# A Strassen-Winograd encoder layer on one core: the plain chunks become pairs, and the gathering bank begins with a copy

## The chip, the core and the metric

The kernel runs on one core of a Trainium2 chip. Its time is the device time of one execution in microseconds (us). TensorE (PE) does the matrix products, into eight PSUM banks of 128 x 512 float32. VectorE (DVE) and ScalarE (ACT) move and combine results, SyncE (SP) and GpSimd (POOL) issue DMAs.

## The reference

One post-norm encoder layer on x of 1024 x 1024, float32:

```
h = LN1(alpha*x + 0.5*SwiGLU_a(x))          # SwiGLU(x) = (silu(x Wg) * (x Wu)) Wd, width 2752
h = LN2(alpha*h + Mixer(h))
h = LN3(alpha*h + 0.5*SwiGLU_b(h))
# Mixer: one projection -> q, k, v (12 heads of 128), Fourier channels, gates;
#   dilated window attention in 3 head groups + FFT over positions and channels,
#   each projected, gated, summed, one output projection
```

## The kernel before

Every large float32 product is made from parts: `split` rounds an operand on ACT ("hi"), DVE subtracts to get the rest ("lo"), and three matmuls (hi hi, hi lo, lo hi) give one. A **product** is 12 matmuls of 128 x 128 by 128 x 512: four slices of a 512-long inner dimension, three matmuls each.

A **pair** is two chunks of 128 weight columns (gate and up, or q and k) against all rows. It is a 2 x 2 block product, made the Strassen-Winograd way with 7 products for 8 (`PROD`): a11 b11, a12 b21, s4 b22, a22 t4, s1 t1, s2 t2, s3 t3. The s are sums of x's blocks, made once per part by `Operand.derive`; the t are sums of the pair's weight blocks, made on DVE by `pair_weights` (t12 and t34). `ORDER` is the order on TensorE: 1, 6, 2, 7, 5, 4, 3. Bank A takes 1 and 2, bank B takes 6, 7 and 4, bank D takes 5 and 3. `pair_sums` copies product 1 to SBUF on ACT (r1, L501) after product 1, and DVE adds it to bank B after product 6 (r2, L505) and after product 7 (r3, L509). `after` finishes a feed-forward pair: silu of bank A (L587), sum of bank B and r1 on DVE (L593), its silu, two subtractions and two multiplications. `pair_out` does the same for the mixer's pairs, where attention runs beside them.

The first two chunks of each feed-forward part are **plain**: 8 products each (`plain`), first four per chunk on the upper half of the rows (a11, a12), then four on the lower half, so that the sums of x are needed only after 18 products. Products 1 and 2 of the first pair stand between the halves. Then come 19 pairs, a 64-column tail, and the down projection (L741, L763), also Strassen-Winograd.

After the first part and after the output projection come layer norms by row tile (`norm_nodes`): deviation and root on ACT (L896, L898), then two DVE passes, (y + mean) * gain (L903) and * 1/std + offset (L907). The row is stored for later and transposed on TensorE; ACT copies the transpose out of PSUM (L382), with 256 columns per instruction, into the blocks of the next operand. The last norm stores to the output, its last row tile in two halves.

A planner (`Flow`) sets the order on each engine while the program is written: TensorE's jobs stand in the order written by hand, and DVE's, ACT's and the queues' instructions are placed by costs, due times (`need`, `lead`) and free buffers: 46 pages of 128 x 1024, 11 halves, 8 banks. `Q` is a load, `S` an ACT and `V` a DVE task, `F` a TensorE step that goes between jobs when ready. Every engine then runs its list in order.

## Time and profile before

| | us |
|---|---|
| median of 3 runs | 2091.3 (2090.82 to 2091.37) |
| profiled execution | 2091.71 |
| its span | 2089.9 |
| TensorE busy | 2071.5 |
| DVE, ACT, POOL busy | 1371.5, 773.3, 237.3 |
| DMA moved | 378.20 MB, mean 181 GB/s |

Busy time of TensorE is that of matmuls as the profile models them. The waits view lists, for an engine, who was waited for: us in total, times, longest. The chain view follows the work that ended last. In the windows view each engine's busy time stands with its count of instructions, then the granted clock as a share, the DMA share and GB/s. A timeline row is start, duration, engine, line, operation, out<-in, and in brackets the idle time before it and what ended it.

### The profile page before, as it was taken

The numbers are of one execution on the slowest core, as the hardware profiler recorded it, in microseconds if no ns is written. First come the engines' busy times: TensorE is split into PE (matmuls) and PEld (weight loads), VectorE is DVE, ScalarE is ACT, GpSimd is POOL, SyncE is SP. The second block draws the span as 40 slices with busy tenths as digits, with TensorE's granted clock in tenths as the row PEclk, the third lists the DMA queues.
The fourth block names the chain that finished last, engine by engine and source line by source line (L and its number), as shares of the span: only waits on it lengthen the run. The fifth ranks groups of instructions, "written<-read, shape, count | busy, mean of one in ns | idle before, by whom it ended". The sixth has DMA issues, their size and how long they took to land.

```text
span 2089.9 us, 25459 instructions
## 1 busy us (share of the span) xinstructions
PE 2071.5 (99%) x9571; PEld 1724.3 (83%) x9571; DVE 1371.5 (66%) x1879; ACT 773.3 (37%) x1181; POOL 237.3 (11%) x415
## 2 busy tenths in 40 slices
PE   9999999999999999999999999999999999999998
PEld 7888888888888888888888888888788888888886
DVE  6766766676675668556666664857766666675566
ACT  4322222355453212444445433225332222245332
POOL 0222111111000010022132101000001001010000
PEclk9999999999999999999999999999999999999999
DMA  4679766499843336567875439432223223267653
GB/s 171 198 215 304 225 179 187 154 335 405 290 165 121 111 111 177 184 152 204 235 177 163 173 131 348 171 122 111 76 91 130 82 91 136 89 233 271 235 179 106
DMA packets 143740, 378.20 MB, mean 181 GB/s; under 512 B 18291, under 2 KB 40563, under 8 KB 143169
## 3 DMA queue, kind: packets, MB, share of 16 engines
q1 hardware_dynamic: 105600, 251.70, 34.3%
q0 software_dynamic: 38016, 124.88, 20.6%
q8 instruction: 75, 1.23, 0.2%
q14 instruction: 49, 0.39, 0.1%
HBM read 288.72 MB, written 145.45 MB: 208 GB/s over the span
## 4 chain that ended last, share of the span: by engine, by line
PE 97%; issue 1%; DVE 1%; ACT 0%; DMA 0%; SPq 0%; DVEq 0%
PE Bb L422 7%; PE Ba L422 7%; PE Aa L422 5%; PE Ab L422 5%; PE Db L422 5%; PE Da L422 5%; PE Bq L422 5%; PE Dq L422 3%; PE Aq L422 3%; PE Bs L422 3%; PE Zb L741 3%; PE Xb L741 3%; PE Za L741 3%; PE Xa L741 3%; PE wo L1910 3%; PE pj L1823 2%
## 5 line engine op out<-in xcount | busy, mean ns | idle before, releaser
L1405 ACT ACTIVATE p<-p,stat 128x192 f32<-128x192 f32 (+2 forms) x96 | 42.3, 442 | 24.7 <-DVE stat L1400 24.0
L533 POOL DMA_DIRECT2D hsba<-r2b x19 | 10.3, 541 | 330.3 <-DVE r2b L603 312.0
L1392 DVE SCALAR_TENSOR_TENSOR p<-sc,bias 128x512 f32<-128x512 f32 (+1 forms) x40 | 24.8, 620 | 27.9 <-PE sc L1378 21.6
L1437 PEld LDWEIGHTS pv<-pT,v 128*128 128x128 f32 (+1 forms) x320 | 37.1, 189 | 5.2
L533 POOL DMA_DIRECT2D hsaa<-r2a x19 | 10.7, 564 | 263.9 <-DVE r2a L603 263.9
L1437 PE MATMUL pv<-pT,v 128*128 128x128 f32 (+1 forms) x320 | 40.6, 289 | 0.0
L501 ACT ACTIVATE r1a<-Aa 128x512 f32<-128x512 f32 x19 | 11.4, 598 | 73.1 <-PE Aa L422 69.0
L509 DVE TENSOR_TENSOR r3q<-Bq,r1q 128x512 f32<-128x512 f32 x12 | 8.3, 691 | 42.6 <-PE Bq L422 42.6
L587 ACT ACTIVATE sgb<-Ab 128x512 f32<-128x512 f32 x19 | 11.4, 598 | 63.8 <-PE Ab L422 63.8
L509 DVE TENSOR_TENSOR r3b<-Bb,r1b 128x512 f32<-128x512 f32 x19 | 13.1, 691 | 32.7 <-PE Bb L422 32.7
L590 DVE TENSOR_TENSOR r3b<-Db,r3b 128x512 f32<-128x512 f32 x19 | 13.1, 691 | 32.5 <-PE Db L422 32.5
L587 ACT ACTIVATE sga<-Aa 128x512 f32<-128x512 f32 x19 | 11.4, 598 | 61.5 <-PE Aa L422 61.5
L1378 PE MATMUL sc<-oq,oq 128*128 128x192 f32 (+2 forms) x192 | 33.8, 322 | 0.0
L590 DVE TENSOR_TENSOR r3a<-Da,r3a 128x512 f32<-128x512 f32 x19 | 13.1, 691 | 28.9 <-PE Da L422 28.8
L1378 PEld LDWEIGHTS sc<-oq,oq 128*128 128x128 f32 x192 | 29.9, 190 | 2.0
L1579 POOL DMA_DIRECT2D comb_t<-stat x48 | 29.1, 613 | 9.9 <-DMA stat<-stat 9.2
L501 ACT ACTIVATE r1b<-Ab 128x512 f32<-128x512 f32 x19 | 11.4, 598 | 47.7 <-PE Ab L422 47.7
L493 DVE TENSOR_TENSOR usa<-ua,usa 128x512 fp32r<-128x512 f32 x19 | 13.1, 692 | 21.0 <-ACT usa L489 20.9
L422 PE MATMUL Db<-Zs40h,usb 128*128 128x512 f32 x76 | 26.5, 389 | 0.0
L422 PE MATMUL Db<-Zs41h,usb 128*128 128x512 f32 x76 | 26.5, 389 | 0.0
L422 PE MATMUL Da<-Xs40h,usa 128*128 128x512 f32 x76 | 26.5, 389 | 0.0
L422 PE MATMUL Da<-Xs41h,usa 128*128 128x512 f32 x76 | 26.5, 389 | 0.0
(7420 smaller groups left out, 7223.7 us busy)
## 6 DMA issues: line engine op xcount, KB each, us to landing
qa<-hsas SPq DMA_DIRECT2D x44, 256.0 KB, 5.4
qa<-tdat SPq DMA_DIRECT2D x44, 256.0 KB, 5.4
qb<-hsbs SPq DMA_DIRECT2D x44, 256.0 KB, 4.6
ga<-in_ffn_gu_dram SPq DMA_DIRECT2D x21, 512.0 KB, 4.3
ua<-in_ffn_gu_dram SPq DMA_DIRECT2D x21, 512.0 KB, 5.5
gb<-in_ffn_gu_dram SPq DMA_DIRECT2D x21, 512.0 KB, 4.1
ub<-in_ffn_gu_dram SPq DMA_DIRECT2D x21, 512.0 KB, 3.6
qa<-hsaa SPq DMA_DIRECT2D x33, 256.0 KB, 5.4
```

The lines of the kernel that those rows point to most:

```text
L422: nc.tensor.matmul(out, pick(w, a)[:, k * P:(k + 1) * P], self.cols(xn, b, k), start=first and k == 0 and ti == 0, stop=last and k == 3 an ...
L501: nc.scalar.activation(H[c, "t1"], B[c, "A"], AF.Copy)
L587: nc.scalar.activation(H[c, "s0"], B.pop((c, "A")), AF.Silu)
L590: nc.vector.tensor_sub(H[c, "t3"], B[c, "D"], H[c, "t3"])
L741: nc.tensor.matmul(B[tag, set_, m], pick(q, a)[:, m * P:(m + 1) * P], pick(q, b)[:, R], start=first and j == 0 and ti == 0, stop=j == PAIR ...
L1378: nc.tensor.matmul(sv[:, i, :], qk[0][:, qt * P:(qt + 1) * P], qk[1][:, k0:k0 + w], start=True, stop=True, skip_group_check=True)
L1392: stt(p3(), sv, scale, bv, op0=OP.mult, op1=OP.add)
L1405: nc.scalar.activation(p3()[:, i, :], p3()[:, i, :], AF.Exp, bias=stats[h][:, k, 0:1], scale=1.0, accum_out=stats[h][:, k, 1:2])
L1437: nc.tensor.matmul(out_of(tiles.index(qt)), env["v"][kc, rows], pt[r0:r0 + rows, sl * P:(sl + 1) * P], start=qt not in seen, stop=last, sk ...
L1579: nc.gpsimd.dma_start(dst, bass.AP(tensor=sd.tensor, offset=sd.offset + 48 * p0 + 2 * col, ap=ap))
L1823: nc.tensor.matmul(bk[hf], pick(wv, a)[:, k, cc * P:(cc + 1) * P], pick(attn[k], b)[:, hf * 512:(hf + 1) * 512], start=(k == 0 and ti == 0 ...
L1910: nc.tensor.matmul(bk[i], pick(merged[k], a)[:, ms], pick(wo[k], b)[:, i * 512:(i + 1) * 512], start=(k == 4 * gi and ti == 0), stop=(k == ...
```

## The change

The plain chunks go: all 21 chunks of a feed-forward part are pairs. `lead_jobs` lets products 1 and 2 of six pairs lead (1 of three, 2 of three, then the other three), with only their gate chunks loaded and split for it, in 0.25 MB pieces; the gate chunk is loaded again for the sums. The other five products of these pairs follow, interleaved. `pair_run` orders the other pairs and those of the mixer: 1, then 3 of the pair before, 6, 2, 7, 5, 4.

`pair_sums` now begins bank B with an ACT copy of product 1 (`seed`), in a bank that an earlier product has filled (`kept_bank`); products 6, 7 and 4 add to it. ACT copies bank B to SBUF after 6 and after 7 where DVE made sums; the sum after 4 is not made any more, since the bank holds it.

Norms 1 and 2 (`norm_tile`) make the row without gain and offset in one ACT pass after a small DVE step; gain and offset per column are put in by the ACT copies after the transposes, now eight of 128 columns for four of 256, from a small array `c_ln`. The row itself with gain and offset, which is needed later for the residual, is made by `norm_rows` during the next pairs: load, two DVE passes, store. Norm 3 (`norm_out`) makes its first pass before the root is there. The loads of x come in an order of their own, the first block in 0.25 MB pieces; four sums of value weights, and two loads of constants, are due later; the planner keeps 4 pages back, not 6.

```diff
-    RATE, LAND, KEEP = 0.28, 2.5, 6
+    RATE, LAND, KEEP = 0.28, 2.5, 4
...
+        if isinstance(need, tuple):
+            def piece(i):
+                cs, last = slice(i * 512, (i + 1) * 512), None
+                def hi_():
+                    if i == 0:
+                        st["h"] = page(name + "h", F32R)
+                    nc.scalar.activation(st["h"][:, cs], get()[:, cs], AF.Copy)
+                def lo_():
+                    if i == 0:
+                        st["l"] = page(name + "l", F32R)
+                        put((st["h"], st["l"]))
+                    nc.vector.tensor_sub(st["l"][:, cs], get()[:, cs], st["h"][:, cs].bitcast(F32))
+                sn = S(0.6, hi_, deps[i], need[i], lead + 1.5, 1.3, pages=0 if i else 2)
+                return V(0.69, lo_, [(sn, 0.1)], need[i], lead, gives=gives if i else 0)
+            return [piece(0), piece(1)]
...
+                        for j in range(2 * i, 2 * i + 2):
+                            k = c0 + 4 * q + j
+                            nc.scalar.activation(self.raw[n, i][:, (j % 2) * 512 + col * P:(j % 2) * 512 + (col + 1) * P],
+                                                 ps[q][:, j, :], AF.Identity, bias=ln_cols[:, k + 8:k + 9],
+                                                 scale=ln_cols[:, k:k + 1])
...
-    ORDER = ((1, "A", 1), (6, "B", 1), (2, "A", 0), (7, "B", 0), (5, "D", 1), (4, "B", 0), (3, "D", 0))
+    BANK = {1: "A", 2: "A", 6: "B", 7: "B", 4: "B", 5: "D", 3: "D"}
     GIVES = {1: 0, 6: 0, 2: 2, 7: 0, 5: 2, 4: 2, 3: 1}
+    KT, AHEAD = {}, set()
...
+    def pair_run(cs, X, fresh, between=None):
+        todo, late = [], None
+        for i, c in enumerate(cs):
+            if i == len(cs) - 1 and between:
+                todo.append(None)
+            if (c, 1) not in J and (c, 1) not in todo:
+                todo.append((c, 1))
+            if late:
+                todo.append(late)
+            if i == 0 and fresh:
+                AHEAD.add(c)
+                todo += [(c, p) for p in (5, 6, 2, 7)] + [(cs[1], 1), (c, 4), (c, 3)]
+            else:
+                todo += [(c, p) for p in (6, 2, 7, 5, 4)]
+                late = c, 3
+        for x in todo + [late]:
+            if x is None:
+                between()
+            else:
+                pair_job(x[0], X, x[1], 4 if x[0] == cs[-1] else 0)
+    def lead_jobs(cs, X, nxt):
+        n = len(cs)
+        todo = [(c, p) for part in (cs[:3], cs[3:]) for p in (1, 2) for c in part]
+        todo += [(cs[0], 5), (cs[0], 6), (cs[1], 5)]
+        for i, c in enumerate(cs):
+            todo += [(c, 5)] if i > 1 else []
+            todo += [(c, 7), (cs[i + 1], 6) if i + 1 < n else (nxt, 1), (c, 4), (c, 3)]
+        AHEAD.update(cs[:2])
+        for c, p in todo:
+            pair_job(c, X, p)
+    def lead_weights(c, w, need, leads=None):
+        def load(i):
+            def run():
+                if i == 0:
+                    W[c, "lead"] = page(f"ld{nm(c)}")
+                nc.sync.dma_start(W[c, "lead"][:, i * 512:(i + 1) * 512], w[c[1], 0][:, i * 512:(i + 1) * 512])
+            return Q(need if leads else J[c, 1 + i], 0.25, run, pages=1 - i, lead=leads[i] if leads else 24.0)
+        split(f"ld{nm(c)}", lambda: W[c, "lead"], lambda p: put(c, ("b11", "b21"), p), [[load(0)], [load(1)]],
+              (J[c, 1], J[c, 2]))
...
-        q0, q1 = pair_load(c, w, 0, j[1]), pair_load(c, w, 1, need1 or j[1])
+        n12 = j[5] if c in AHEAD else j[6]
+        t0 = n12 if lead else j[1]
+        q0, q1 = pair_load(c, w, 0, t0), pair_load(c, w, 1, t0)
...
-    def pair_sums(c):
+    def pair_sums(c, src, lead=False):
+        tile_, free = src
 
         def t1():
-            H[c, "t1"] = half(f"r1{nm(c)}")
+            t = page(f"rs{nm(c)}")
+            H[c, "t1"], H[c, "s0"] = t[:, L], t[:, R]
             nc.scalar.activation(H[c, "t1"], B[c, "A"], AF.Copy)
 
-        def t2():
-            H[c, "t2"] = half(f"r2{nm(c)}")
-            nc.vector.tensor_add(H[c, "t2"], B[c, "B"], H[c, "t1"])
-        def t3():
-            H[c, "t3"] = half(f"r3{nm(c)}")
-            nc.vector.tensor_add(H[c, "t3"], B[c, "B"], H[c, "t1"])
-        n1 = S(0.62, t1, [J[c, 1]], J[c, 2], halves=1)
-        n2 = V(0.69, t2, [n1, J[c, 6]], J[c, 7], halves=1)
-        n3 = V(0.69, t3, [n1, J[c, 7]], J[c, 4], halves=1)
-        return n1, n2, n3
+        def seed():
+            B[c, "B"] = tile_()
+            nc.scalar.activation(B[c, "B"], H[c, "t1"] if lead else B[c, "A"], AF.Copy)
+        def keep(t):
+            def run():
+                H[c, t] = half(f"{t}{nm(c)}")
+                nc.scalar.activation(H[c, t], B[c, "B"], AF.Copy)
+            return run
+        n1 = S(0.62, t1, [J[c, 1]], J[c, 2], pages=1) if lead else J[c, 1]
+        n1 = S(0.62, seed, [n1] + free, J[c, 6], tail=0.4)
+        if not lead:
+            J[c, 2].after(n1)
+        return S(0.62, keep("t2"), [J[c, 6]], J[c, 7], halves=1), S(0.62, keep("t3"), [J[c, 7]], J[c, 4], halves=1)
+    def kept_bank(c, bk):
+        return lambda: KT[c, bk][0], [KT[c, bk][1]]
+    def give_bank(c, bk):
+        t = B.pop((c, bk))
+        if (c, bk) in KT:
+            KT[c, bk][0] = t
+        return t
+    def keep_bank(c, bk, node):
+        if (c, bk) in KT:
+            KT[c, bk][1] = node
...
-            ns = S(0.62, s0, [J[c, 2]], frees=1, halves=1)
+            ns = S(0.62, s0, [J[c, 2]], frees=int((c, "A") not in KT), halves=0 if lead else 1)
+            keep_bank(c, "A", ns)
+            src = kept_bank(*((c, "A") if i < 2 else (ck[i - 2], "B") if i <= LEAD else (ck[i - 1], "A")))
+            n2, n3 = pair_sums(c, src, lead)
             n4 = V(0.69, u1, [J[c, 5], n3], J[c, 3])
-            n5 = V(0.69, g1, [J[c, 4], n3, n2], frees=1)
-            n6 = S(0.65, g1s, [n5])
+            n6 = S(0.65, g1s, [J[c, 4], n3], frees=int((c, "B") not in KT), halves=0 if lead else 1)
+            keep_bank(c, "B", n6)
             n7 = V(0.69, u0, [J[c, 3], n2], frees=1)
-            return [V(0.69, h0, [n7, ns], hgives=1), V(0.69, h1, [n6, n4], hgives=1)]
+            out = [V(0.69, h0, [n7, ns], hgives=0 if lead else 1), V(0.69, h1, [n6, n4], hgives=0 if lead else 1)]
+            if lead:
+                S(0.0, lambda: None, out, gives=1)
+            return out
...
-        for hf in range(2):
-            for c, which, i in ([(c, w, i) for c in range(PL) for w in range(2) for i in range(2)] if hf == 0 else
-                                [(c, w, i) for i in range(2) for c in range(PL) for w in range(2)]):
-                J[ck[c], which, hf, i] = job(12 * MM, plain(ck[c], hf, which, i), 1 - i, gives=2 if hf and i else 0)
-                J[ck[c], which, hf] = J[ck[c], which, hf, i]
-            if hf == 0:
-                pair_job(ck[PL], X, 1, "A", 1)
-                pair_job(ck[PL], X, 2, "A", 0)
-            else:
-                J[ck[PL - 1], 1, 1, 0].back["p"] += 4
-        for c in range(PL, NFULL):
-            if c == NFULL - 1:
-                for hf in range(2):
-                    J[tl, hf] = job(24 * MM, tail_half(hf), 1, gives=4 * hf)
-            pair_jobs(ck[c], X, c == NFULL - 1)
+        lead_jobs(ck[:LEAD], X, ck[LEAD])
+        def tails():
+            for hf in range(2):
+                J[tl, hf] = job(24 * MM, tail_half(hf), 1, gives=4 * hf)
+        pair_run(ck[LEAD:], X, False, tails)
 
         c0 = ck[0]
-        first = {"a11": J[c0, 0, 0, 0], "a12": J[c0, 0, 0, 1], "a21": J[c0, 0, 1, 0], "a22": J[c0, 0, 1, 1]}
+        first = {"a11": J[c0, 1], "a12": J[c0, 2], "a21": None, "a22": J[c0, 4]}
         if callable(X.got):
-            X.got = X.got(first)
-        X.derive(first, {p: J[ck[PL], p] for p in PROD}, 30.0)
-        for c in ck[:PL]:
-            n0, n1 = J[c, 0, 0, 0], J[c, 1, 0, 0]
-            pair_split(c, "g", 0, ("b11", "b21"), [pair_load(c, w_gu, 0, n0)], n0)
-            pair_split(c, "u", 1, ("b12", "b22"), [pair_load(c, w_gu, 1, n1)], n1)
-            hidden(c, [swi_plain(c, hf) for hf in range(2)])
+            X.got = X.got(J[c0, 1])
+        X.derive(first, {p: J[c0, p] for p in PROD}, 30.0)
+        for i, c in enumerate(ck[:LEAD]):
+            lead_weights(c, w_gu, J[c0, 1], ((41.0 if i == 0 else 38.6 - 0.2 * i), 37.0 - 0.2 * i) if tag == "a" else None)
...
+        n = V(0.12, mean, deps)
+        return st, n, S(1.7, dev, [n], pages=1)
+    def norm_tile(acc, sums, deps, name, which):
+        st, _, n = norm_head(acc, sums, deps, name, which)
+        def shift():
+            nc.vector.reciprocal(st["rs"], st["rs"])
+            nc.vector.tensor_mul(sums()[:, 2:3], sums()[:, 2:3], st["rs"])
+        def scaled():
+            nc.scalar.activation(st["y"], st["a"], AF.Identity, bias=sums()[:, 2:3], scale=st["rs"])
+        n = V(0.3, shift, [n])
+        return S(1.08, scaled, [n], gives=1), lambda: st["y"]
+    def norm_rows(which, m, src, deps, dst, need):
+        st = {}
+        def load():
+            st["y"] = page(f"n{which}{m}")
+            nc.sync.dma_start(st["y"], src)
+        def gain():
+            nc.vector.tensor_mul(st["y"], st["y"], LN[which][0])
+        def offset():
+            nc.vector.tensor_add(st["y"], st["y"], LN[which][1])
+        n = V(1.22, gain, [Q(need, 0.5, load, deps, 10.0, pages=1)], slack=40.0)
+        NORM[which].append(n)
+        n = V(1.22, offset, [n], slack=40.0)
+        n = S(0.0, lambda: nc.gpsimd.dma_start(dst, st["y"]), [n])
+        fl.later(n, 5.0, gives=1 if m < 7 else 3)
+        return n
...
+    def norm_out(m, acc, sums, deps, parts, store):
...
+        f = [V(0.12 + 1.1 / parts, begin, [n], pages=1)]
+        f += [V(0.12 + 1.1 / parts, lambda cs=cs: first(cs), [f[0]]) for cs in cols[1:]]
+        for cs in cols:
+            n = V(0.12 + 1.1 / parts, lambda cs=cs: second(cs), [r] + f)
...
-        for n, (hf, kh) in (("a11", (0, 0)), ("a12", (0, 1)), ("a21", (1, 0)), ("a22", (1, 1))):
+        for n, (hf, kh), at in (("a11", (0, 0), 40.0), ("a12", (0, 1), 38.0), ("a22", (1, 1), 35.0), ("a21", (1, 0), 34.0)):
             for i in range(2):
-                def load(n=n, i=i, hf=hf, kh=kh):
-                    X1.raw[n, i] = t = page(f"x{n}{i}")
-                    nc.sync.dma_start(t, xt[hf, kh, :, i * 1024:(i + 1) * 1024])
-                got[n, i] = [Q(first[n], 0.5, load, pages=1)]
+                def load(j, w, n=n, i=i, hf=hf, kh=kh):
+                    if j == 0:
+                        X1.raw[n, i] = page(f"x{n}{i}")
+                    nc.sync.dma_start(X1.raw[n, i][:, j:j + w], xt[hf, kh, :, i * 1024 + j:i * 1024 + j + w])
+                if n == "a11":
+                    got[n, i] = tuple([Q(need, 0.25, lambda j=j, load=load: load(j * 512, 512), pages=1 - j,
+                                         lead=at - 0.2 * (2 * i + j))] for j in range(2))
+                else:
+                    got[n, i] = [Q(need, 0.5, lambda load=load: load(0, 1024), pages=1, lead=at - 0.2 * i)]
...
     def norm1(m, acc, sums, deps):
-        n, y = norm_nodes(m, acc, sums, deps, f"y1_{m}", 1)
-        spilled[1, m] = S(0.0, lambda: nc.gpsimd.dma_start(y_spill[m], y()), [n])
-        X2.turn(m, n, y)
+        n, y = norm_tile(acc, sums, deps, f"y1_{m}", 1)
+        unit[1, m] = S(0.0, lambda: nc.gpsimd.dma_start(n_spill[m], y()), [n])
+        X2.turn(m, n, y, 0)
...
-        pair_jobs(PC[c], X2, i == len(pairs) - 1)
+    pair_run([PC[c] for c in pairs], X2, True)
...
+        src = kept_bank("v", "D") if c == PC[pairs[0]] else kept_bank(PC[pairs[c[1] - 1]], "A")
+        if c != PC[pairs[-1]]:
+            KT[c, "A"] = [None, None]
...
+        def o21():
+            nc.scalar.activation(views(pages_[0], 1), views(B.pop((c, "B")), None), kind, bias=bias[0], scale=1.0)
...
+        n = S(0.69, o11, [J[c, 2]], frees=int((c, "A") not in KT), pages=2)
+        keep_bank(c, "A", n)
+        n2, n3 = pair_sums(c, src)
+        nodes = [[n, S(0.69, o21, [J[c, 4], n3, n], frees=1)], []]
...
+    for m in range(8):
+        spilled[1, m] = norm_rows(1, m, n_spill[m], [(unit[1, m], 5.0)], y_spill[m], J[PC["q", m + 3], 1])
+    ln_consts(1, ln1_g, ln1_b, J[PC["q", 3], 1])
...
+        n, y = norm_tile(lambda st=st: st["a"], lambda sums=sums: sums, deps, f"y2_{m}", 2)
+        unit[2, m] = S(0.0, lambda m=m, y=y: nc.gpsimd.dma_start(n2_spill[m], y()), [n])
+        X3.turn(m, n, y, 16)
```

More of the change, by code (lines that the diff above doesn't have):

```diff
@@ L520, in ffn @@
         TAIL = FF - NFULL * P
[L521 to L530 removed]
+        LEAD = 6
         def spill(name, j, t):
@@ L882, in ln_consts, with norm_head @@
             n.after(q)
-    def norm_nodes(m, acc, sums, deps, name, which, parts=1, store=None):
+    def norm_head(acc, sums, deps, name, which):
         st = {}
@@ L901, in first, with begin, second @@
+    def norm_out(m, acc, sums, deps, parts, store):
+        st, n, r = norm_head(acc, sums, deps, f"y3_{m}", 3)
+        w = D // parts
+        cols = [slice(i * w, (i + 1) * w) for i in range(parts)]
+        def first(cs):
+            a = st["a"][:, cs]
+            stt(st["z"][:, cs], a, sums()[:, 2:3], LN[3][0][:, cs], op0=OP.add, op1=OP.mult)
+        def begin():
+            st["z"] = page(f"z3_{m}")
+            first(cols[0])
+        def second(cs):
             if cs.start == 0:
                 nc.vector.reciprocal(st["rs"], st["rs"])
-            stt(st["y"][:, cs], st["a"][:, cs], sums()[:, 2:3], LN[which][0][:, cs], op0=OP.add, op1=OP.mult)
@@ L905, in second @@
-        def second(cs):
-            y = st["y"][:, cs]
-            stt(y, y, st["rs"], LN[which][1][:, cs], op0=OP.mult, op1=OP.add)
-            if store is not None:
-                store(m, cs, y)
-        n = V(0.12, mean, deps)
-        NORM[which].append(n)
-        n = S(1.4, dev, [n], pages=1)
-        w = D // parts
-        for i in range(parts):
-            cs = slice(i * w, (i + 1) * w)
-            n = V(0.15 + 1.1 / parts, lambda cs=cs: first(cs), [n], gives=1 if i == parts - 1 else 0)
-            n = V(0.12 + 1.1 / parts, lambda cs=cs: second(cs), [n])
```

141 lines of the change are left out of this document (72 added, 69 removed).

## The prediction

> **What bounds the kernel now.** I read the page first, then the waits of TensorE, then the chain of waits, then stretches.
>
> ```profile
> PE 2071.5 (99%) x9571; PEld 1724.3 (83%) x9571; DVE 1371.5 (66%) x1879; ACT 773.3 (37%) x1181; POOL 237.3 (11%) x415
> PE 97%; issue 1%; DVE 1%; ACT 0%; DMA 0%; SPq 0%; DVEq 0%
> PE ga L422 <- ACT ga0h L330: 2.9, 1, 2.9
> PE tpZ L373 <- DVE y L907: 1.7, 1, 1.7
> PE Ba L422 <- DVE r2a L505: 1.2, 1, 1.2
> PE Bb L422 <- DVE r2b L505: 0.9, 1, 0.9
> PE Aa L422 <- ACT r1a L501: 0.7, 1, 0.7
> PE Ab L422 <- ACT r1b L501: 0.7, 1, 0.7
> ```
>
> TensorE is busy for 2071.5 of 2089.9 us; 18.4 us are idle. The waits name where they lie: once at the start, once before a transpose, and four times in the first pair of each feed-forward part. No other pair shows a wait above these, though DVE makes two sums per pair between products. So time is matmuls times their pitch, plus a short list of single stalls. The chain gives the pitch:
>
> ```profile
> 28.10 5.44 PE ua L422 x24
> 33.54 2.73 PE Aa L422 x12
> 36.94 3.02 PE Aa L422 x12
> ```
>
> A product of 12 matmuls takes 5.44 / 2 = 2.72 us (0.227 us each). The second row pair shows a stall: product 1 ends at 36.27, product 2 begins at 36.94 (0.67 us) and takes 3.02, 0.30 more than 2.72.
>
> **The change part by part.** The profiled execution took 2091.7 us, 1.8 beside its span; the median of the runs is 2091.3. Sums are made against 2091.7. About 0.2% (4 us) is what can be told from no change.
>
> *Products.* A plain chunk is 8 products, a pair 7. Each feed-forward part had 2 plain chunks and 19 pairs (149 products) and gets 21 pairs (147). Over both parts 4 products go: 4 x 2.72 = **-10.9 us**. TensorE is the bound, so this counts in full. The tail, values, projections and transposes keep their counts.
>
> *The start.*
>
> ```profile
> 1.39 3.93 PE L1944 MATMUL warm<-ident 128*128 128x128 f32 x20 [1.39 <-DVE eps L310]
> 4.58 1.06 ACT L330 ACTIVATE Xa110h<-xa 128x1024 fp32r<-128x1024 f32 x1 [2.56 <-DMA xa<-in_xt_dram]
> 7.09 1.06 ACT L330 ACTIVATE ga0h<-ga 128x1024 fp32r<-128x1024 f32 x1 [0.22 <-DMA ga<-in_ffn_gu_dram]
> 8.20 0.79 PE L422 MATMUL ga<-Xa110h,ga0h 128*128 128x512 f32 x1 [2.88 <-ACT ga0h L330]
> 11.34 0.63 PE L422 MATMUL ga<-Xa111h,ga0h 128*128 128x512 f32 x1
> 11.76 0.63 PE L422 MATMUL ga<-Xa111l,ga0h 128*128 128x512 f32 x1
> 15.02 0.39 PE L422 MATMUL ga<-Xa120h,ga0h 128*128 128x512 f32 x1
> 15.24 0.39 PE L422 MATMUL ga<-Xa120l,ga0h 128*128 128x512 f32 x1
> ```
>
> Weights are third in the queue, behind 1 MB of x. The change puts the first 0.25 MB of weights first and cuts x and weights into 0.25 MB pieces, each rounded on ACT in half the 1.06. The first 0.5 MB landed at 4.58; it will now hold both operands. The second piece's rounding (0.53) ends at about 5.2, so the first matmul is at 5.2 to 6, I take 5.6: **-2.6** (bounds -4, if pieces land in proportion, and 0, if small pieces land no sooner).
>
> The matmuls begin 0.42 us apart at 11.3 and 0.22 apart at 15: over the 6.5 us from 8.2 on some 15 of them lose 0.2 each, 3 us. Either as many half-rate matmuls follow (0), or the warm-up, which would now run into the products without the 2.88 us gap, counts: 3.93 / 0.42 = 9 fewer are at half rate (-1.8). I take the middle, **-0.8**. [...]
>
> *The first pair.* The stall between products 1 and 2 goes, because products 1 of three chunks precede the first product 2: 2 x (0.67 + 0.30) = **-1.9**. The waits on r2 (1.2 and 0.9, with 0.25 slower products behind) go as well, since DVE no longer makes this sum: **-2.6**. What is late next there is the operand sums, below.
>
> *The turn into the second feed-forward part.*
>
> ```profile
> 1410.60 1.28 DVE L903 SCALAR_TENSOR_TENSOR y<-ya,lw,ln2g 128x1024 f32<-128x1024 f32 x1
> 1411.92 1.28 DVE L907 SCALAR_TENSOR_TENSOR y<-y,lnrs,ln2b 128x1024 f32<-128x1024 f32 x1
> 1413.95 1.21 ACT L382 ACTIVATE Za<-tpZ 128x256 f32<-128x256 f32 x4 [3.48 <-PE tpZ L373]
> 1440.00:1450.00 10.00, 10.00 (x45) 8.25 (x44) 9.91 (x16) 6.12 (x11) 0.53 (x1) 1.00 0.53 199
> ```
>
> Two DVE passes (2.6 us with their gaps) become one ACT pass (1.05 to 1.15, by the full-page passes) and a 0.3 us DVE step: the stalled transpose is ready 1.3 us sooner, **-1.3**. Gain and offset move into the evacuation: 8 small ACT instructions for 4. Four of 256 columns took 1.21, so eight of 128 take 1.2 to 2.4. ACT gains about 2 us per row of 6.4 us; it was 6.1 of 10 busy beside a DVE at 9.9, so it has room, and DVE gets 2.6 us per row back. The row form is made later: 8 stores, 8 loads, 8 stores per norm on the SP and POOL queues, and two DVE passes, in the pair stages, where
>
> ```profile
> 1000.00:1050.00 50.00, 50.00 (x270) 42.23 (x269) 32.89 (x44) 22.15 (x61) 8.71 (x15) 1.00 0.80 222
> q1 hardware_dynamic: 105600, 251.70, 34.3%
> ```
>
> DVE has a third free, and each pair loses three DVE steps. With the second load of six gate chunks per part, DMA gains about 22 MB on 378. I cost all this at nothing; uncovered, the 16 x 2.5 us of DVE would be 40.
>
> *The end.*
>
> ```profile
> 2083.70 0.16 DVE L902 RECIPROCAL lnrs<-lnrs 128x1 f32<-128x1 f32 x1 [1.64 <-ACT lnrs L898]
> 2083.78 0.73 DVE L903 SCALAR_TENSOR_TENSOR y<-yb,lsb,ln3g 128x512 f32<-128x512 f32 x1
> 2085.22 0.75 DVE L903 SCALAR_TENSOR_TENSOR y<-yb,lsb,ln3g 128x512 f32<-128x512 f32 x1
> ```
>
> Four half passes followed the reciprocal; the two of L903 now run while ACT squares, 1.64 us in which DVE sat idle: 2 x 0.75 = **-1.5**.
>
> *The gathering bank (64 pairs).* Bank B is begun with an ACT copy of product 1, so product 6 waits for it. One product (2.72 us) is put between, also between 6 and 7 and between 7 and 4, where two further ACT copies must fit.
>
> ```profile
> L501 ACT ACTIVATE r1a<-Aa 128x512 f32<-128x512 f32 x19 | 11.4, 598 | 73.1 <-PE Aa L422 69.0
> 214.25 0.60 ACT L501 ACTIVATE r1a<-Aa 128x512 f32<-128x512 f32 x1 [4.08 <-PE Aa L422]
> 964.67 0.40 ACT L1405 ACTIVATE p<-p,stat 128x128 f32<-128x128 f32 x1 [1.29 <-DVE stat L1400]
> 967.38 0.39 ACT L1405 ACTIVATE p<-p,stat 128x128 f32<-128x128 f32 x1
> ```
>
> The nearest copy takes 0.60 and in the feed-forward ACT idles some 4 us ahead of it, so it starts at the product's end. No ACT row writes a PSUM bank; between 0.5 and 1.0 us I take 0.6. That leaves 2 us of slack, hence nothing in the feed-forward. In the attention stage a train of 8 exps holds ACT from 964.67 to 967.8, 3.1 us: a copy behind all of it comes 1.0 to 1.2 us late. Few will; I take **+1.5** (0 to 23).
>
> *The opening.* The sums of X are needed after 12 products where they had 18, 16.3 us sooner.
>
> ```profile
> 28.63 1.05 ACT L330 ACTIVATE Xa220h<-xa 128x1024 fp32r<-128x1024 f32 x1
> 33.65 0.69 DVE L577 SCALAR_TENSOR_TENSOR sga<-sga,ua 128x512 f32<-128x512 f32 x1 [6.86 <-PE ua L422]
> 34.25 1.22 DVE L334 TENSOR_TENSOR Xa220l<-xa,Xa220h 128x1024 fp32r<-128x1024 f32 x1
> 61.60 1.23 DVE L334 TENSOR_TENSOR Xs40l<-xa,Xs40h 128x1024 fp32r<-128x1024 f32 x1 [1.12 <-ACT Xs41h L330]
> 10.00:20.00 10.00, 10.00 (x35) 7.98 (x34) 6.07 (x6) 7.53 (x9) 0.00 (x0) 0.76 1.14 462
> ```
>
> From 33.65 to 62.8, 29 us, DVE made the X sums, their parts and one pair's weights. Now all this is needed by the 19th product: 5.6 + 18 x 2.72 + 2.4 of half clock = 57. Added ahead of it are the second pair's weights and the last leads, about 10 us by passes of the same lengths, so 39 in all. x and the leads are 7 MB; at 0.46 MB/us after the first half MB at 4.6 they are there at about 19. 57 - 19 = 38 us against 39: **+2** in the first part (0 to 12). In the second part the same list meets a DVE that got 2.6 us per row back: **+1.5** (0 to 6). That DVE entry that waited 6.86 us for TensorE (and kept Xa220l, whose input was there at 29.7) is not in the new order: the leads have no DVE work behind products.
>
> Sum: -10.9 -2.6 -0.8 -1.9 -2.6 -1.3 -1.5 = -21.6, and +1.5 +2 +1.5 = +5: 2091.7 - 16.6 = **2075.1 us**.
>
> **The rivals.**
>
> *Late copies in the attention stage* (slower). ACT gets three copies per pair there with a deadline of one product each, where before one copy had two. If the exp trains are ahead of them as a rule, the 36 copies of 12 pairs come up to 1.2 us late each, 43 us; at half, 22. 2091.7 - 21.6 + 22 + 3.5 = 2095.6. It decides from about 0.6 us per copy. For it: ACT has 22 of 50 us busy there and gains some 4 (1.9 per pair). Against: no pair in that stage waits today, and DVE kept the same kind of deadline at 33 of 50. [...]
>
> *A starved opening.* If DVE begins the X sums no sooner than at 33.65, whether for pages or for queue order, 29 us and the second pair's 6 end at 69 against 57: 12 us in the first part, half in the second. 2091.7 - 21.6 + 18 + 1.5 = 2089.6, no change. For it: two 0.9 to 1.2 us stalls stood there already. Against: data are there at 19.
>
> *No new wait at all.* 2091.7 - 21.6 = 2070.1. For it: the pairs run without waits today. Against: the opening's accounts balance to within 1 us.
>
> **How the numbers follow.** Forecast 0.58, no new wait 0.18, starved opening 0.12, late copies 0.12. The forecast's own range is 2071 to 2081. The range of 2067 to 2089 holds it, no new wait with a gate that opens early and a first matmul at the lower bound (2070.1 - 1.0 - 1.4 = 2067.7), and most of a starved opening; late copies are left out. A starved opening goes 0.07 to faster, 0.03 to same, 0.02 to slower, late copies 0.01 to same and 0.11 to slower: faster 0.83, same 0.04, slower 0.13.
>
> **What would show it.** 9523 matmuls for 9571. First matmul of a product at 5.2 to 6, 6 to 15 matmuls at half rate. No wait of product 2 on r1. Any wait of A, B or D products on the X parts or on t12 splits lies in the first 60 us of a part and sums to under 8 us. Waits of B products on the copies of product 1 stay under 3 us in all, ACT rows writing B banks at 0.5 to 1.0 us. Two half passes after the last reciprocal. Wrong would be: waits of Bq products on ACT in most attention pairs; a first product stalled by 5 us or more on an X sum; or a first matmul later than 7.

## The result, and the profile after

The changed kernel takes 2091.48 us (median of 14 runs, 2087.94 to 2094.79) against 2091.35 for the kernel before (14 runs, 2090.45 to 2092.65): ratio 1.0001, 95% interval 0.9994 to 1.0009. No change can be measured. Forecast were 2075.1, in a range of 2067 to 2089.

The head of the page of the kernel after, and TensorE's waits in it (us in total, times, longest):

```profile
PE 2065.3 (99%) x9523; PEld 1715.0 (82%) x9523; DVE 1276.3 (61%) x1757; ACT 906.5 (43%) x1437; POOL 246.8 (12%) x432
```

```profile
PE Aa L447 <- ACT t3a L585: 6.2, 1, 6.2
PE pt L1558 <- ACT p L1542: 4.2, 5, 1.4
PE tpZ L392 <- ACT y L985: 1.7, 5, 0.6
PE Db L447 <- DVE t3b L669: 1.1, 1, 1.1
PE pv L1574 <- ACT pT L1563: 0.4, 1, 0.4
```

The 48 matmuls are gone, and so are the waits on r1 and r2. The two largest entries are new: one wait of 6.2 us in the first feed-forward part, and five of the attention transposes `pt` on the exponentials. Neither stands in the list of before.

Where the time went shows best when the span is cut between the stages (at the first matmul of each, for the mixer's pairs at their last; times from the traces; the last three columns are experiments told below):

| stage, us | before | after | after, sums early and reserve 6 | before, sums moved | before, reserve 4 |
|---|---|---|---|---|---|
| first matmul of a product | 8.2 | 6.0 | 6.1 | 8.7 | 8.4 |
| gates and ups of the first feed-forward | 423.4 | 422.3 | 417.2 | 430.7 | 423.4 |
| its down products, values | 336.7 | 336.2 | 336.2 | 336.8 | 337.4 |
| pairs of the mixer, with attention | 505.3 | 515.3 | 505.6 | 505.3 | 516.5 |
| projections, output | 177.6 | 178.7 | 178.7 | 177.6 | 177.6 |
| gates and ups of the second feed-forward | 420.2 | 414.1 | 414.2 | 420.2 | 420.2 |
| its down products | 209.6 | 209.6 | 209.6 | 209.6 | 209.6 |
| after the last matmul | 8.9 | 7.3 | 7.8 | 8.9 | 8.9 |
| span | 2089.9 | 2089.4 | 2075.4 | 2097.8 | 2102.0 |

After against before: the start gives 2.2, the second feed-forward part 6.1, the end 1.5. The first feed-forward part gives 1.2, though its twin gives 6.1 for the same edit. The mixer's pairs take 9.9 back. So two places hold the lost time.

*First place.* Timelines of the kernel after, of SP's queue, POOL and ACT; then two windows, where the granted clock is the third number from the end:

```profile
193.19 0.49 SPq L772 DMA_DIRECT2D tdat<-in_ffn_down_dram  x1
214.64 0.89 POOL L1178 DMA_DIRECT2D vtt<-in_in_values_dram  x1 [0.29 <-DMA w_rev<-rev]
228.74 0.47 SPq L1175 DMA_DIRECT2D vtt<-vtt  x1
229.32 0.51 SPq L521 DMA_DIRECT2D ga<-in_ffn_gu_dram  x1
226.51 0.60 ACT L666 ACTIVATE sga<-Aa 128x512 f32<-128x512 f32 x1 [1.60 <-PE Aa L447]
236.48 1.06 ACT L331 ACTIVATE ga12h<-ga 128x1024 fp32r<-128x1024 f32 x1 [9.38 <-DMA ga<-in_ffn_gu_dram]
237.45 0.58 ACT L585 ACTIVATE t3a<-Aa 128x512 f32<-128x512 f32 x1
```

```profile
236.30:243.00 6.70, 4.92 (x12) 3.85 (x13) 3.64 (x5) 2.60 (x3) 0.00 (x0) 0.50 1.04 343
243.20:250.00 6.80, 6.80 (x31) 5.60 (x31) 4.68 (x7) 3.21 (x4) 0.00 (x0) 1.00 1.16 354
```

Read it backwards. TensorE waits for the copy t3a at 237.45. That copy stood in ACT's list behind the split of the gate weights ga12, which waited 9.38 us for its load. That load was issued at 229.32, right behind a copy of the value-weight sums (`vtt`), and SP issued nothing between the load at 193.19 and that copy at 228.74. The copy reads what an add issued on POOL at 214.64 writes; the add landed 14.1 us later, and the copy was issued at once. So a copy that nobody needs for hundreds of microseconds held the queue in which the next weights stood. After the wait TensorE ran at half the clock (0.50 granted up to 243): the matmuls began 0.43 us apart instead of 0.23 for some ten of them, so the event cost about 8.8 us and not 6.2 (141 matmuls from 220 to 260 us, where 40 us without a wait hold 180). The second place shows the same behind shorter waits.

*Second place.* Timelines of the kernel after, of ACT near 859, of DVE near 996, and of DVE, ACT and TensorE near 1080; then the window behind:

```profile
858.77 0.63 ACT L561 ACTIVATE usq<-uq 128x512 fp32r<-128x512 f32 x1 [3.21 <-PE Aq L447]
...
996.65 0.69 DVE L1766 TENSOR_TENSOR pw<-pw,cb 128x512 f32<-128x512 f32 x1 [4.01 <-DMA cb<-comb]
...
1077.96 0.69 DVE L1766 TENSOR_TENSOR pw<-pw,cb 128x512 f32<-128x512 f32 x1 [5.44 <-DMA cb<-comb]
1079.29 0.68 DVE L1529 SCALAR_TENSOR_TENSOR p<-sc,bias 128x512 f32<-128x512 f32 x1
...
1082.81 0.51 ACT L1542 ACTIVATE p<-p,stat 128x256 f32<-128x256 f32 x1 [4.24 <-DVE stat L1537]
1083.46 0.93 PE L1558 MATMUL pt<-ident,p 128*128 128x128 f32 x4 [1.06 <-ACT p L1542]
```

```profile
1086.30:1089.50 3.20, 3.20 (x9) 2.43 (x9) 3.06 (x8) 2.00 (x4) 0.06 (x1) 0.50 0.09 13
```

At 996 and 1078 DVE stands 4.01 and 5.44 us before a multiplication that needs the broadcast cb, and the scores' next step waits behind it in DVE's list, then the exponential on ACT, then the transpose. At 859 ACT stands 3.21 us before a weight split (usq) whose page TensorE still reads, with exponentials behind it. The broadcast for the step at 996 was issued at 990.88 and took 5.7 us to land. In both cases an early step of something else is at the head of the list, and what stands behind it is not taken first: the next scores were done at 995.26 and 1075.14, and DVE took them at 997.98 and 1079.29; at 859 the statistics were done by 857.82, and ACT began the exponentials at 859.30. Of the five waits, three (1.9 us) lie behind the broadcast, in pairs 9 and 12, and two (2.3 us) behind a weight split, in pairs 4 and 6. After the two waits of pair 12, 1.06 and 0.54 us, the granted clock was 0.50 for over 3 us, as the last row shows. TensorE had waited for 1.6 us in all there, for 6.2 in the first place, so in this trace shorter waits were followed by half clock too.

### The profile page after: what moved, and what is told of

It reads as the page before. It is cut to its first block, busy times and chain, and to the rows that moved or that the text cites. A ratio compares the mean times of both kernels' runs of the same rounds, so it can differ in the third digit from the quotient of the medians.

```text
span 2089.4 us, 25573 instructions
## 1 busy us (share of the span) xinstructions
PE 2065.3 (99%) x9523; PEld 1715.0 (82%) x9523; DVE 1276.3 (61%) x1757; ACT 906.5 (43%) x1437; POOL 246.8 (12%) x432
## 4 chain that ended last, share of the span: by engine, by line
PE 89%; issue 3%; DMA 3%; ACT 3%; DVE 1%; POOL 1%; SPq 0%; DVEq 0%; POOLq 0%
PE Ab L447 13%; PE Aa L447 13%; PE Aq L447 6%; PE Db L447 5%; PE Da L447 5%; PE As L447 5%; PE Zb L812 3%; PE Xb L812 3%; PE Za L812 3%; PE Xa L812 3%; PE Dq L447 2%; PE pj L1964 2%; PE v L1214 2%; PE Ds L447 2%; PE vB L1153 2%
## 5 line engine op out<-in xcount | busy, mean ns | idle before, releaser
L616 POOL DMA_DIRECT2D hsaa<-t2a x21 | 11.9, 569 | 316.0 <-DVE t2a L681 302.8
L616 POOL DMA_DIRECT2D hsba<-t2b x21 | 11.4, 543 | 281.1 <-DVE t2b L681 274.6
L677 DVE TENSOR_TENSOR t2b<-Db,t2b 128x512 f32<-128x512 f32 x21 | 14.5, 691 | 44.5 <-PE Db L447 44.5
L585 ACT ACTIVATE t2a<-Aa 128x512 f32<-128x512 f32 x21 | 12.6, 600 | 62.8 <-PE Aa L447 62.7
L677 DVE TENSOR_TENSOR t2a<-Da,t2a 128x512 f32<-128x512 f32 x21 | 14.5, 691 | 39.9 <-PE Da L447 39.9
L585 ACT ACTIVATE t2b<-Ab 128x512 f32<-128x512 f32 x21 | 12.6, 598 | 60.6 <-PE Ab L447 60.6
L1334 DVE SCALAR_TENSOR_TENSOR oq<-Dq,b_cols,t2q 128x512 f32<-128x512 f32 x12 | 11.8, 983 | 42.2 <-PE Dq L447 42.2
L1720 POOL DMA_DIRECT2D comb_t<-stat x48 | 29.3, 616 | 14.1 <-DMA tdbt<-in_ffn_down_dram 5.3
L669 DVE TENSOR_TENSOR t3a<-Da,t3a 128x512 f32<-128x512 f32 x21 | 14.5, 690 | 25.5 <-PE Da L447 19.5
L669 DVE TENSOR_TENSOR t3b<-Db,t3b 128x512 f32<-128x512 f32 x21 | 14.5, 690 | 21.9 <-PE Db L447 16.0
L1558 PE MATMUL pt<-ident,p 128*128 128x128 f32 x140 | 22.0, 280 | 4.7 <-ACT p L1542 4.2
```

Source lines behind the costliest of these rows:

```text
L585: nc.scalar.activation(H[c, t], B[c, "B"], AF.Copy)
L669: nc.vector.tensor_sub(H[c, "t3"], B[c, "D"], H[c, "t3"])
L677: nc.vector.tensor_sub(H[c, "t2"], B.pop((c, "D")), H[c, "t2"])
L1720: nc.gpsimd.dma_start(dst, bass.AP(tensor=sd.tensor, offset=sd.offset + 48 * p0 + 2 * col, ap=ap))
```

## The experiments

Two edits were suspected for the first place (the moved value sums, the new order of pairs) and several for the second: the copies of bank B on ACT, the kept bank, the rows of the first norm, and the reserve of pages (KEEP), which went from 6 to 4. Each ratio is to the kernel before, with its 95% interval. Its median in the shared runs was 2091.94 (first four experiments), 2091.19 (next four) and 2091.36 (last four).

**Value sums early.**

```diff
-        n = Q(J[("a", 7 + i), 1], 1.0, copy, ...)
-        vtn[to] = Q(J[("a", 8 + i), 5], 1.0, add, [n], lead=0.0)
+        n = Q(J[("a", 2 + i), 1], 1.0, copy, ...)
+        vtn[to] = Q(J[("a", 3 + i), 5], 1.0, add, [n], lead=0.0)
```

> The four sums of value weights get the due times that they had before the change (pairs 2 to 6 of the first part, not 7 to 11). Theory Q (queue): the one TensorE wait of 6.2 us at 220 us, with 2.6 us of half-clock matmuls behind it, comes from a value-weight copy that SyncE's queue held until a GpSimd add had landed at 228.7, with the weight loads of the next pairs behind it. Then the stall goes and the time falls by 6 to 9 us against the changed kernel, to about 2083, unless the 8 MB now collide with the opening loads (then up to 5 us come back in the first 60 us). Rival: the loads are late for lack of free buffers; then a stall of several us stays near 220 us and the time is within 2 us of 2091.5.

2083.53 us, ratio 0.9963 (0.9950 to 0.9975). The stall at 220 us is gone, and the first feed-forward part takes 415.0 us in the profiled run (one of 2079.57 us).

**Rows of the first norm made in the last pairs.**

```diff
-        spilled[1, m] = norm_rows(1, m, ..., J[PC["q", m + 3], 1])
-    ln_consts(1, ln1_g, ln1_b, J[PC["q", 3], 1])
+        spilled[1, m] = norm_rows(1, m, ..., J[PC["s", m], 1])
+    ln_consts(1, ln1_g, ln1_b, J[PC["s", 0], 1])
```

> The row form of norm 1 (8 loads, 16 DVE passes, 8 stores) is due in the gate pairs and not in the attention pairs. The mixer's pairs lost 9.9 us against the kernel before (515.1 for 505.2), nearly all as TensorE waiting for attention transposes on ACT's exponentials. Theory R (rows): the stores and passes hold up GpSimd's queue and DVE, so the statistics and the exponentials come late; then the pairs fall to 505 to 509 us and the time to about 2083 to 2087. Theory A (copies on ACT): the waits come from ACT's three copies per pair; then the pairs stay at 512 to 517 us.

2083.76 us, ratio 0.9962 (0.9948 to 0.9976). The mixer's pairs take 506.9 us, the wait at 220 us stays. This seemed to convict the rows; the reserve experiments below show that it was half the truth.

**Copies of bank B on DVE in the attention pairs.**

```diff
-                nc.scalar.activation(H[c, t], B[c, "B"], AF.Copy)
+                if c[0] == "q":
+                    nc.vector.tensor_copy(H[c, t], B[c, "B"])
+                else:
+                    nc.scalar.activation(H[c, t], B[c, "B"], AF.Copy)
```

> In the 12 attention pairs the two copies of the gathering bank (after products 6 and 7) are made by DVE, 0.69 us each, where ACT made them. Theory A (copies on ACT): a copy at the head of ACT's queue waits for its product while ready exponentials stand behind it; without two of three copies the transposes' waits of 9 us fall to 3 or less, the mixer's pairs to 505 to 508 us, the time to about 2083 to 2085. Theories R (rows) and P (pages that are given out too soon): the pairs stay within 3 us of 515.

2103.19 us, ratio 1.0057 (1.0040 to 1.0073); pairs 525.7 us, 10.4 more than in the kernel after. Taking work from ACT did not help: the transposes' waits rose from 4.2 to 7.5 us. But over half of the loss lies behind the attention, in the mixer's later pairs, as one wait of TensorE with a lower clock around it (0.91 granted in the mean from 1160 to 1180 us, 1.00 there in the kernel after):

```profile
PE As L447 <- ACT t3s L588: 4.1, 1, 4.1
```

```profile
1165.39 0.69 DVE L1770 TENSOR_TENSOR pw<-pw,cb 128x512 f32<-128x512 f32 x1 [5.91 <-DMA cb<-comb]
1168.22 1.06 ACT L331 ACTIVATE t12s16h<-t12s 128x1024 fp32r<-128x1024 f32 x1 [7.17 <-DMA cb<-comb]
1169.19 0.58 ACT L588 ACTIVATE t3s<-As 128x512 f32<-128x512 f32 x1
```

DVE stands before the broadcast again, the weight sums behind it come late, ACT waits to split them, and the copy t3s stands behind the split.

**The old scheme in the attention pairs** (a fresh bank B, its sums made by DVE).

```diff
-            if p in (1, 5):
+            if p in new:        # (1, 5, 6) in the attention pairs
...
+            nc.vector.tensor_add(H[c, t], B[c, "B"], H[c, "t1"])
```

> The 12 attention pairs alone go back to the scheme of before: bank B begun by product 6, one ACT copy of product 1, the sums and the third output on DVE; the order of products stays the new one. Theory A (copies on ACT) and a theory B (the bank that is held between pairs leaves one less for attention): the pairs fall to 505 to 507 us, the time to about 2082. If with DVE copies the loss stays and here it goes, it is B. Theories R and P: the pairs stay within 3 us of 515, since rows and pages are as in the changed kernel.

2100.05 us, ratio 1.0045 (1.0028 to 1.0061); pairs 521.5 us, 6.2 more than in the kernel after. This too is one wait behind the attention, of the same kind (0.83 granted in the mean from 1160 to 1180 us):

```profile
PE As L447 <- ACT t3s L601: 4.9, 1, 4.9
```

```profile
1161.68 0.69 DVE L1792 TENSOR_TENSOR pw<-pw,cb 128x512 f32<-128x512 f32 x1 [6.77 <-DMA cb<-comb]
```

The attention pairs themselves took as long as with the gathering bank, to about 1 us, with transposes' waits of 4.6 us for 4.2. So neither the copies nor the kept bank took the time. Both this run and the one before it had the reserve of 4.

**Both undone: sums early and rows late** (the two edits above together).

> Both moves together: value-weight sums due as before the change, row form of norm 1 due in the gate pairs. If the two losses are separate, as the two single runs say (8.4 and 8.2 us under the kernel before), they add: about 2075.5, with no wait near 220 us and the pairs at 506 to 508 us. If one was only passing its loss on to the other, the time stays at 2080 to 2084.

2078.47 us, ratio 0.9931 (0.9914 to 0.9948). The two gains add up but for some 3 us (2075.5 was expected): in the profiled run a wait of 1.8 us for t12a5 stands at 104 us in the opening.

**Rows loaded and stored without the two DVE passes.** The stored row of the first norm lacks gain and offset here; the rows of the second keep their passes.

```diff
-        n = V(1.22, gain, [Q(need, 0.5, load, deps, 10.0, pages=1)], slack=40.0)
-        n = V(1.22, offset, [n], slack=40.0)
+        q = Q(need, 0.5, load, deps, 10.0, pages=1)
+        if which == 1:
+            n = S(0.0, lambda: None, [q], slack=40.0)
...
```

> The changed kernel with the row form of norm 1 where it is, in the attention pairs, but its two DVE passes left out: the row is loaded and stored again without gain and offset (the part of the computation that is left out). Loads, stores, pages and constants stay. If DVE's 20 us of passes make the statistics late (theory R by DVE), the pairs fall from 515 to about 507 us and the time to about 2083. If it is the stores on GpSimd's queue, the loads or the pages that the rows hold, the pairs stay at 512 to 516 us.

2087.85 us, ratio 0.9983 (0.9974 to 0.9993); pairs 510.9 us. It does not decide: the run with the sums early kept the passes and had 510.7 us in the same pairs. The stage's length depends by some 4 us on how the lists happen to fall.

**Rows late, sums among the down products.**

```diff
+        n = Q(J["a", "d", 3, 3 * i], 1.0, copy, ...)
+        vtn[to] = Q(J["a", "d", 7, 3 * i], 1.0, add, [n], lead=0.0)
```

> As the run with both moves, but the value-weight sums go the other way, into the down projection's last products (548 to 610 us), far from the sums of down weights. Theory Q by collision (two chains of copy and add share SyncE's and GpSimd's queues between pairs 7 and 18, and each waits for the other's landing): no wait near 220 us here either, 2074 to 2078. If the early place itself is what helped, a stall of 5 us or more returns somewhere in the first part or at the values, over 2080.

2082.26 us, ratio 0.9956 (0.9939 to 0.9973). The first feed-forward part is free (413.4 us), but a new wait stands before the first norm's transposes; TensorE's wait, and ACT's and SP's lists around it, in this kernel:

```profile
PE tpY L392 <- ACT y L985: 4.0, 1, 4.0
```

```profile
572.13 1.06 ACT L331 ACTIVATE qa41h<-qa 128x1024 fp32r<-128x1024 f32 x1 [4.37 <-PE Va L812]
574.85 1.06 ACT L331 ACTIVATE qa42h<-qa 128x1024 fp32r<-128x1024 f32 x1 [1.66 <-PE Va L812]
575.82 1.14 ACT L970 ACTIVATE y<-ya,lsa 128x1024 f32<-128x1024 f32 x1
583.50 0.42 SPq L801 DMA_DIRECT2D qa<-tdat  x1
599.04 0.48 SPq L1175 DMA_DIRECT2D vtt<-vtt  x1
```

SP issues nothing for 15 us ahead of the copy, but only from 583.9 on, and TensorE's wait was over at 584.2; no wait of TensorE follows from that stand. The transposes were late because ACT began the norm (L970) behind two weight splits that waited for TensorE: 156.2 us after the first down product, 150.7 in the kernel after. Why the splits stand later in this list was not traced. Down products and values take 341.7 us there (336.2 in the kernel after), 5.5 longer. So the later place is no cure, though not for the reason of theory Q.

**Reserve back at 6.**

```diff
-    RATE, LAND, KEEP = 0.28, 2.5, 4
+    RATE, LAND, KEEP = 0.28, 2.5, 6
```

> The changed kernel with 6 free pages held back from early loads in place of 4, and nothing else. Theory P (pages given out in the plan just before TensorE has really released them make ACT and DVE wait at the head of their queues): the transposes' waits of 7 to 9 us fall by half or more, the pairs to 510 or less. Theories Q and R: both losses stay, the time within 3 us of 2091.5.

2087.40 us, ratio 0.9981 (0.9972 to 0.9991). The pairs take 506.7 us with every row of the norm in place. The first feed-forward part gets longer (426.9): its wait on t3a is 8.4 us, and in the opening of each part 1.0 us of new waits on weight splits appears. In the pairs this is what theory P expected; of the five waits of the transposes, though, its mechanism fits only the two behind weight splits.

Four runs then set the rows against the reserve, and tried each of the two edits alone on the kernel before.

**Both undone and reserve 6.**

> The changed kernel with the value-weight sums due early, the rows of the first norm made in the last pairs, and the planner's reserve of free pages (KEEP) back at 6. Theory K (rows in the attention pairs cost time only because, with a reserve of 4, loads not yet due take the pages that split weights wait for): with the rows gone from there the reserve matters little; mixer pairs 505 to 508 us, time 2076 to 2080, at most 2 us under the same kernel with KEEP 4 (2078.5). Theory R (rows cost there by their own work whatever the reserve): the same here. If the reserve of 6 costs the opening of the first feed-forward part, as the 2 us of waits on t12a3 in the KEEP 6 run suggest, the first part is about 417 to 419 us.

2077.99 us, ratio 0.9936 (0.9923 to 0.9950); first feed-forward 416.7 us, pairs 508.6.

**Sums early and reserve 6, rows where the change has them.**

> The changed kernel with the value-weight sums due early and KEEP 6; the rows of the first norm stay in the attention pairs. Theory K: mixer pairs 506 to 508 us, the stall at 220 us gone, time about 2079 (the KEEP 6 run's 2087.4 less 8.4). Theory R: mixer pairs about 511 us, as with the sums early and KEEP 4, time 2083 to 2084.

2078.04 us, ratio 0.9945 (0.9931 to 0.9958); pairs 505.6 us. This is the third column of figures in the table. Rows in the attention pairs cost nothing measurable here: the kernel without them there is no faster. Theory R is out. TensorE's waits in this kernel, the four largest:

```profile
PE tpZ L392 <- ACT y L985: 1.7, 5, 0.6
PE warm L2089 <- DVE eps L311: 1.4, 1, 1.4
PE Aa L447 <- DVE t12a2l L335: 0.6, 1, 0.6
PE Aa L447 <- ACT Xa110h L346: 0.6, 1, 0.6
```

**The kernel before, value sums moved** (the reverse of the first diff).

> The kernel before with one edit: the four value-weight sums due at pairs 7 to 10 and 8 to 11 instead of 2 to 5 and 3 to 6. Theory Q (a copy of these sums holds SP's queue until the add before it has landed, and weight loads stand behind it): one wait of 4 to 9 us in the middle of the first feed-forward part, then half-clock matmuls, time 2096 to 2102. Rival (the stall comes from the new order of the pairs, and the sums only met it): no such wait, time within 2 us of the kernel before.

2099.54 us, ratio 1.0042 (1.0028 to 1.0056): 8.2 us slower by this edit alone, in a kernel with the old order of pairs. POOL, SP's queue, ACT and TensorE's wait in it:

```profile
220.52 0.89 POOL L1054 DMA_DIRECT2D vtt<-in_in_values_dram  x1 [3.66 <-DMA vtt<-in_in_values_dram]
234.96 0.48 SPq L1051 DMA_DIRECT2D vtt<-vtt  x1
235.61 0.45 SPq L452 DMA_DIRECT2D ga<-in_ffn_gu_dram  x1
245.14 1.06 ACT L330 ACTIVATE ga12h<-ga 128x1024 fp32r<-128x1024 f32 x1 [6.44 <-DMA ga<-in_ffn_gu_dram]
```

```profile
PE Ba L422 <- DVE r3a L509: 4.6, 1, 4.6
```

The same chain at the same pair: add, 14.4 us, copy, gate weights, split. Theory Q holds; the new order of the pairs has no part in it.

**The kernel before, reserve 4.**

> The kernel before with one edit: KEEP 4 for 6. Theory K: this kernel loads no rows for a norm in the attention pairs, so few loads that are not yet due compete there; mixer pairs 505 to 508 us, time within 3 us of the kernel before. Rival (the smaller reserve delays split weights by itself): waits of the transposes on the exponentials as in the changed kernel, mixer pairs 510 to 515, time 2096 to 2101.

2102.86 us, ratio 1.0053 (1.0039 to 1.0067): 11.5 us slower by one number. It fell where the rival put it, with 516.5 us in the mixer's pairs, somewhat more than the rival's 510 to 515. DVE's waits in those pairs and two rows of its timeline, for this kernel; then the same waits line for the kernel before and for the one with sums early and reserve 6:

```profile
DVE pw L1625 <- DMA cb<-comb: 21.1, 5, 7.1
```

```profile
996.45 0.69 DVE L1625 TENSOR_TENSOR pw<-pw,cb 128x512 f32<-128x512 f32 x1 [5.47 <-DMA cb<-comb]
1081.32 0.69 DVE L1625 TENSOR_TENSOR pw<-pw,cb 128x512 f32<-128x512 f32 x1 [7.06 <-DMA cb<-comb]
```

```profile
DVE pw L1625 <- DMA cb<-comb: 6.1, 2, 3.1
```

```profile
DVE pw L1766 <- DMA cb<-comb: 2.9, 2, 2.3
```

The transposes wait there in pairs 9 and 12, 6.7 us in all, where three of the five waits of the kernel after stand, behind the same multiplication. My theory K expected no such loss without rows, and is wrong in this half: rows are not needed for it. What remains is that the smaller reserve changes the order that the planner writes in these pairs, so that a step whose broadcast has just been issued stands ahead of the scores. Moving the rows out writes yet another order, in which that step happens to stand elsewhere.

How the reserve leads to exactly this order stays open: which load takes which page sooner was not traced. That the two runs with the copies or the bank undone grew by 6 to 10 us fits it: both ran with the reserve of 4, and each met one more long wait behind the broadcast. Neither was run with the reserve of 6.

## Why the prediction was wrong

The step that failed is the cost of what is moved. It said "I cost all this at nothing" of loads and rows, which came out, but it left two edits of the diff out of the sum without a word: the four value sums due later and the reserve of pages. Alone, on the kernel before, they cost 8.2 and 11.5 us; undoing them in the changed kernel brings it from 2091.48 to 2078.04. The rest of the sum was forecast at 2075.1, so the remaining error is 2.9 us. Point by point, by the run with sums early and reserve 6, where the two losses are gone:

- **Products**: 9523 matmuls, as said. Each feed-forward part should give 5.45 us by them.
- **Start**: first matmul at 5.96 us in the kernel after, for a forecast of 5.2 to 6; 2.2 us for 2.6.
- **Clock**: underrated. The first products of the kernel after, and the granted clock (third number from the end) in the kernel before, two windows, and in the kernel after:

```profile
5.96 0.50 PE L447 MATMUL Aa<-Xa110h,lda0h 128*128 128x512 f32 x1 [0.83 <-ACT Xa110h L346]
6.69 0.50 PE L447 MATMUL Aa<-Xa110l,lda0h 128*128 128x512 f32 x1 [0.23 <-DVE Xa110l L352]
```

```profile
4.60:7.90 3.30, 0.72 (x7) 0.48 (x5) 2.22 (x2) 2.91 (x3) 0.00 (x0) 1.00 0.99 353
8.00:14.70 6.70, 6.46 (x14) 4.63 (x15) 5.53 (x6) 4.89 (x6) 0.00 (x0) 0.50 1.02 405
```

```profile
4.20:16.00 11.80, 10.69 (x47) 7.50 (x45) 8.31 (x12) 9.42 (x16) 0.00 (x0) 1.00 1.04 383
```

  Before, the granted clock was 1.00 in the gap behind the warm-up, from 4.6 to 7.9 us, and 0.50 from 8.0 to 14.7, when the products had begun. After, with a gap of 0.83 us for 2.88, it stays at 1.00 from 4.2 to 16.0: no matmul runs at half rate, where 6 to 15 were expected, and the first ones are spread by waits for their operands instead. Matmuls up to 20 us lose 1.6 us against their full pitch, 3.4 before; so 1.8 came for the 0.8 taken. The forecast's larger figure, 1.8 for 9 fewer at half rate, is that number, but partly by luck: 14 matmuls ran at half rate before and none after, and the new waits took part of it back. The range's "gate that opens early" was the author's estimate: no run shows a gate as such, only that the granted clock was 1.00 for the first products, where it had been 0.50.
- **First pair**: the waits on r1 and r2 are gone, as said.
- **Opening**: no wait between 16 and 220 us in the kernel after. With the reserve of 6, in the run with the sums early, 1.6 us of waits on the splits of t12a2 and t12a3 appear, and 1.0 of t12b2 in the second part. Forecast were +2 and +1.5. The feed-forward parts as a whole: forecast -6.7 and -6.1 (products, clock, first pair, opening), measured -6.2 and -5.9, of which 1.0 in the second is only a shift of transposes across the cut (see the turn).
- **Gathering bank**: the copies that begin a bank,

```profile
L580 ACT ACTIVATE Aa<-Aa 128x512 f32<-128x512 f32 x15 | 8.7, 582 | 23.2 <-PE Aa L447 23.2
L580 ACT ACTIVATE Aq<-Aq 128x512 f32<-128x512 f32 x11 | 6.4, 582 | 16.0 <-PE Aq L447 16.0
```

  take 0.58 us for the 0.6 taken. No product of the attention pairs waits for one. The pairs come out 0.3 us above before (forecast +1.5).
- **Turn into the second part**: wrong. Five waits of the transposes, 0.2 to 0.6 us each, make 1.7 in all, which is what the single stall cost before. The ACT pass takes longer than the 1.05 to 1.15 assumed:

```profile
L985 ACT ACTIVATE y<-ya,lw,lnrs 128x1024 f32<-128x1024 f32 x8 | 9.9, 1238 | 1.7 <-DVE lw L982 1.7
```

  So the turn gave nothing, for -1.3. That the stage of projections and output is 1.1 us longer is no further loss: 56 of the 64 transposes stand ahead of its end, where 48 stood, and the eight take 1.0 us.
- **End**: 1.5 us in the kernel after, as said (1.1 with the sums early and reserve 6).
- **Rows of the norm**: nothing, in the end as forecast. With the reserve of 6 the kernel with them in the attention pairs and the one without (2078.04 and 2077.99) cannot be told apart.

The rival "late copies in the attention stage" had one of the two stages and, by chance, nearly the right time (2095.6), but its mechanism is refuted: the exponentials were late, not the copies behind them. The rival "a starved opening" came nearest (2089.6, no change), and that is luck too: between 16 and 220 us, where it put its 12 us, TensorE did not wait. The expected signs of failure, waits of Bq products on ACT and a product stalled on an X sum, did not appear.

The best version measured is the change with value sums early and a reserve of 6 (2078.04), level with the one that also moves the rows (2077.99).

## What to carry to other kernels

Price every line of a diff that changes when something is issued, even when its transfer has hundreds of microseconds to spare: ask what stands behind it in the same queue, and whether it must itself wait there. A planner's constant is an edit to all lists that it writes, so test it alone on the kernel before. An experiment that gives the time back does not yet name the cause: moving the rows helped, and the rows cost nothing.

## What the runs showed of the hardware

In the kernel after, a wait of 6.2 us of TensorE in mid-kernel was followed by some ten matmuls at half rate (0.43 us apart for 0.23, granted clock 0.50 up to 243 us), so it cost 2.6 us more than it shows in the waits view. Two shorter waits close together, 1.06 and 0.54 us, were followed by seven such matmuls (0.50 from 1086.3 to 1089.5). Around the waits of 6.9 to 8.1 us near 230 us in three experiments (rows late, copies on DVE, old scheme) the granted clock was 0.86 to 0.92 in the mean of each 20 us from 220 to 260, for 1.00 with the sums early, where there is no such wait.

Four accumulating adds from DRAM to DRAM, issued on POOL, took long to land: 8.2 to 16.5 us in the kernel before, 14.1 to 21.4 in the kernel after. One copy that reads the result of such an add stood in SP's list until it had landed: SP issued nothing for 35.5 us, from 193.19 to 228.74, the last 14.1 of them behind the add's issue.
